# Adding the two softmaxes of a differential attention inside PSUM instead of on VectorE

## The chip, the cores and the metric

One core of a Trainium2 chip runs the whole program. The metric is the device time of one execution in microseconds (us). Of the kernel before there are three timed runs, with a median of 3167.21 us (3165.14 to 3172.83), and one profiled execution.

## The reference

The program is one inference step of a two-layer decoder whose mixer has four parallel branches. This document is about branch A, differential attention over the 2048 tokens of the prompt, with 4 heads. Each head has two queries and two keys of 32 dimensions and one value of 64:

```
def probs(q, k):
    s = einsum('bqhd,bkhd->bhqk', q, k) * scale
    return softmax(where(visible, s, NEG_BIG), axis=-1)
p = probs(q1, k1) - lam * probs(q2, k2)
return einsum('bhqk,bkhd->bqhd', p, v)
```

The result is normalised by its root mean square over the 64 values, multiplied by a gate, and goes with the other three branches through an output projection (1024 by 1024) and a LayerNorm.

## The kernel before

Each of the two layers runs in two stages. The first makes all projections and the branches B, C and D, and writes queries, keys and values of A to DRAM scratch. The second stage is `attention` together with `out_tile`, the output projection. The second stage is what the change touches.

**Tiles.** The 2048 queries are 16 query tiles of 128. They go in blocks of 4, 4, 4, 2 and 2 tiles; within a block the loops run over 4 heads and then over the tiles of the block. A query tile number qi sees qi + 1 key tiles of 128, so a head has 1 + 2 + ... + 16 = 136 pairs of query tile and key tile, and the program has 136 x 4 heads x 2 layers = 1088. There are 16 x 4 x 2 = 128 calls of `attn_probs`, one per layer, head and query tile. A call with more than 8 key tiles works in two pieces (a first piece of 1024 keys, and the rest); 64 of the 128 calls do.

**attn_probs**, for each of the two softmaxes (m = 0, 1) and each piece: TensorE forms the scores in PSUM (L678, with a mask matmul L680 on the diagonal), VectorE takes the row maximum (L682, and L684 takes the smaller of the negated maxima of both pieces), ScalarE takes the exponential into an SBUF tile P1 or P2 with the row sum beside it (L686). The rows are not divided by their sum: since the output is normalised afterwards, only the ratio of the two sums matters, and VectorE forms it as one factor per row, r = -lam * l1 / l2 (L697, L698). Where there are two pieces, the first one needs a further factor per row, col(0, 5) for m = 0 and col(1, 5) for m = 1 (L691). Then the two tiles are added on VectorE into P1: for the last piece P1 += r * P2 (L712); for the first of two pieces ScalarE scales P2 (L706, after a one-column product L702) and VectorE adds it to the scaled P1 (L707).

**attn_value** takes P1 in groups of up to 4 key tiles. TensorE transposes each 128 x 128 part into PSUM (L725, `nc.tensor.transpose` with the identity), ScalarE copies the group to SBUF (L727), and TensorE multiplies it with the values into an accumulator (L730, on one of two 64-column halves of the array). After the last tile of a block TensorE adds the two halves (L741) and the head is normalised.

**Order.** `attention` emits `attn_probs` of a tile before `attn_value` of the tile before it, so one tile's probabilities are in the making while the last one's are multiplied. After a block's attention the program emits `out_tile` for the tiles of the block before (L1373 to L1375, three fp32r matmuls for each of 8 parts and 2 halves). A scheduler of the framework then fixes the order of each engine's instructions; each engine works through its own list in order. The P1 tiles come from 5 buffers and the P2 tiles from 3 (`NP1`, `NP2`), the scores from two PSUM buffers of 1024 columns, the transposed groups from two PSUM banks. A buffer is taken again when its last reader is done.

Of the kernel before, what the change touches and what calls it, by code (L numbers as in the profile page):

```python
# [9 lines left out]
F32 = mybir.dt.float32  # L10
# [4 lines left out]
AF = mybir.ActivationFunctionType  # L15
ALU = mybir.AluOpType
# [8 lines left out]
P = 128  # L25
# [43 lines left out]
def hymba_step_kernel(  # L69
# [9 lines left out]
    nc = tc.nc  # L79
# [9 lines left out]
    RW = TG + NS  # L89
    NB = TG // 512  # L90

    KN = dict(zs=5, ms=2, os=4, NK=5, NMW=8, APO='o k p2 h p1 v v0 op q', ORD0='g10 n1 g2 b4 g4 n1', ORD1='g8 n2',
              NPH=2, NP1=5, NP2=3, LEAD=1, KD0=0, KD1=1, LO0=2, LO1=2, ZIP=0, WF=0, RUN=1, QB=0, RB=0, RC=0, RD=1, RS=1,
              RA=0, RO=0, GP=1, CI=1, CS=0, MO=0, PT=300, PSA=0, PN=1000, PB=0, PG=0, PD=1000, PBV=0, PCZ=0, PGB=0,
              POUT=-500, PATT=0, PMOD=0, PW=0, PAV=0, PDZ=3000, PQK=500, PSL=0, PSLD=0, PPR=0, PPB=0, OT=1, GO=0, DO=0,
              EP2=0, ECB=0, EPH=0, EAS=0, EAV=0, EDV=0, EOH=0, EOL=1, EOT=1, ESH=0, ESL=1, EQK=1, EDN=1, EAN=1, EDB=1,
# [8 lines left out]

    pick = lambda k: nc.gpsimd if KN[k] else nc.vector

    def cpy(k, out, in_):

        (nc.vector.tensor_copy if KN[k] else nc.scalar.copy)(out, in_)  # L110
    NST = dict(zs=KN['zs'], ms=KN['ms'], os=KN['os'])
    NK, NMW, NPH, NP1, NP2, LEAD = (KN[k] for k in ('NK', 'NMW', 'NPH', 'NP1', 'NP2', 'LEAD'))
    APO, ORD0, ORD1 = (KN[k].split() for k in ('APO', 'ORD0', 'ORD1'))
    PT, PSA, PN, PB, PG = (KN[k] for k in ('PT', 'PSA', 'PN', 'PB', 'PG'))

# [18 lines left out]
    def nm(s):  # L134
        uid[0] += 1
        return f"{s}_{uid[0]}"
# [4 lines left out]
    def St():  # L141
        return pS.tile([P, 1024], F32, tag="S", name=nm("S"))

    def Tt():
        pool.t2 = not pool.t2
        return (pool.T2 if pool.T2 and pool.t2 else pT).tile([P, 512], F32, tag="T", name=nm("T"))
# [4 lines left out]
    def st(tag, dt=F32):  # L151

        return stp.tile([P, 512], dt, tag=tag, name=nm(tag), bufs=NST[tag])
# [4 lines left out]
    def sm(who, kind="", bufs=4):  # L158
        n = SW[who]
        return smp.tile([P, n], I32 if kind == "i" else F32, tag="sm" + who + kind, name=nm("sm" + who + kind), bufs=bufs)  # L160
# [39 lines left out]
    ident = cst[:, C_ID:C_ID + 128]  # L200
# [462 lines left out]
    def attn_probs(qi, qt, kst, l1, Lx, ap):  # L663

        nk = qi + 1
        npc = -(-nk // 8)
        stt = smp.tile([P, 16], F32, tag="stt", name=nm("stt"), bufs=3)
        Pm = []
        sizes = [min(8, nk - k0) * P for k0 in range(0, nk, 8)]
        col = lambda m, j: stt[:, m * 8 + j:m * 8 + j + 1]  # L670
        for m in range(2):
            pms = []
            for pc, n in enumerate(sizes):
                s = St()
                for o in range(0, n, 512):
                    w = min(512, n - o)
                    diag = pc == npc - 1 and o + 512 >= n
                    nc.tensor.matmul(s[:, o:o + w], qt[:, m, :], kst[pc * 2 + o // 512][:, m, 0:w], start=True, stop=not diag)  # L678
                    if diag:
                        nc.tensor.matmul(s[:, o + w - P:o + w], identb, cmaskb, start=False, stop=True)  # L680

                nc.vector.tensor_reduce(col(m, pc), s[:, :n], AX.X, ALU.max, negate=True)  # L682
                if pc:
                    nc.vector.tensor_tensor(col(m, pc), col(m, pc), col(m, 0), ALU.min)  # L684
                p = (ap.p1, ap.p2)[m].tile([P, 1024], F32, tag=("P1", "P2")[m], name=nm("P"), bufs=(NP1, NP2)[m])
                nc.scalar.activation(p[:, :n], s[:, :n], AF.Exp, bias=col(m, pc), scale=1.0, accum_out=l1 if m == 0 and npc == 1 else col(m, 2 + pc))  # L686
                pms.append(p)
            lt = l1 if m == 0 and npc == 1 else col(m, 2)
            if npc > 1:

                nc.scalar.activation(col(m, 5), col(m, 0), AF.Exp, bias=col(m, 1), scale=-1.0)  # L691
                lt = col(m, 6) if m else l1
                nc.vector.scalar_tensor_tensor(lt, col(m, 2), col(m, 5), col(m, 3), op0=ALU.mult, op1=ALU.add)
            Pm.append((pms, lt))
        (p1s, lt1), (p2s, lt2) = Pm
        r = col(0, 7)
        nc.vector.reciprocal(r, lt2)  # L697
        nc.vector.scalar_tensor_tensor(r, lt1, Lx.nlam, r, op0=ALU.mult, op1=ALU.mult)  # L698
        for pc, n in enumerate(sizes):
            p1, p2 = p1s[pc], p2s[pc]  # L700
            if pc == 0 and npc > 1:
                nc.vector.tensor_tensor(col(1, 7), col(1, 5), r, ALU.mult)  # L702
                if KN['EP2']:
                    nc.gpsimd.tensor_scalar(p2[:, :n], p2[:, :n], col(1, 7), None, op0=ALU.mult)
                else:
                    nc.scalar.activation(p2[:, :n], p2[:, :n], AF.Copy, scale=col(1, 7))  # L706
                nc.vector.scalar_tensor_tensor(p1[:, :n], p1[:, :n], col(0, 5), p2[:, :n], op0=ALU.mult, op1=ALU.add)  # L707
            elif n <= KN['ECB'] * P:
                nc.scalar.activation(p2[:, :n], p2[:, :n], AF.Copy, scale=r)
                nc.gpsimd.tensor_tensor(p1[:, :n], p1[:, :n], p2[:, :n], ALU.add)  # L710
            else:
                nc.vector.scalar_tensor_tensor(p1[:, :n], p2[:, :n], r, p1[:, :n], op0=ALU.mult, op1=ALU.add)  # L712
        return p1s

    def attn_value(qi, pm, vst, acc, ls, j4, nt, hd, act, Lx, l, ap):

        nk = qi + 1
        hs = slice(hd * 64, (hd + 1) * 64)
        for c in range(0, nk, 4):
            n = min(4, nk - c)  # L720
            p1 = pm[c // 8]
            o = (c % 8) * P
            pt = Tt()
            for j in range(n):
                nc.tensor.transpose(pt[:, j * P:(j + 1) * P], p1[:, o + j * P:o + (j + 1) * P], ident)  # L725
            ph = ap.h.tile([P, 4, P], F32, tag="ph", name=nm("ph"), bufs=NPH)
            (nc.vector.tensor_copy if n <= KN['EPH'] else nc.scalar.copy)(ph[:, 0:n].rearrange("p k q -> p (k q)"), pt[:, 0:n * P])  # L727
            for j in range(n):
                e = (c + j) % 2
                nc.tensor.matmul(acc[e * 64:(e + 1) * 64, j4 * P:(j4 + 1) * P], vst[c // 4][:, j, hs], ph[:, j, :],  # L730
                                 start=(c + j < 2), stop=(c + j >= nk - 2), tile_position=(0, e * 64))
        if nk == 1:
            nc.vector.memset(acc[64:128, 0:P], 0.0)
        if j4 < nt - 1:
            return
        asb = ap.o.tile([P, 512], F32, tag="asb", name=nm("asb"), bufs=1)
        cpy('EAS', asb[:, 0:nt * P], acc[:, 0:nt * P])

        pt = Tt()
        for j in range(nt):  # L740
            nc.tensor.matmul(pt[:, j * 64:(j + 1) * 64], asb[:, j * P:(j + 1) * P], diagm, start=True, stop=True)  # L741
        ot = ap.o.tile([P, 4, 64], F32, tag="ot", name=nm("ot"), bufs=1)[:, 0:nt]
        nc.scalar.copy(ot, pt[:, 0:nt * 64].rearrange("p (a v) -> p a v", v=64))
        sq = st("ms")[:, 0:nt * 64].rearrange("p (a b) -> p a b", b=64)
        nc.scalar.activation(sq, ot, AF.Square)
        ss, l2, lt = sm("a")[:, 0:nt], sm("a")[:, 0:nt], ls[:, 0:nt]
        nc.vector.tensor_reduce(ss, sq, AX.X, ALU.add)
        nc.vector.scalar_tensor_tensor(l2, lt, EPS, lt, op0=ALU.mult, op1=ALU.mult)
        nc.vector.scalar_tensor_tensor(ss, ss, 1.0 / 64.0, l2, op0=ALU.mult, op1=ALU.add)
        ss = rsqrt(ss, P, nt, "a", KN["RA"] and act is None)  # L750
        on3 = st("ms")[:, 0:nt * 64].rearrange("p (a b) -> p a b", b=64)
        nc.vector.tensor_tensor(on3, ot, ss.unsqueeze(2).to_broadcast([P, nt, 64]), ALU.mult)
        if act is not None:
            nc.vector.tensor_tensor(act[:, :, hs], on3, Lx.ag.unsqueeze(1).to_broadcast([P, nt, 64]), ALU.mult)
            return
        pick('EAN').tensor_tensor(on3, on3, Lx.ag.unsqueeze(1).to_broadcast([P, nt, 64]), ALU.mult)
        store(tok_rows(scr[l].cat, qi - nt + 1, nt)[:, hd * 64:(hd + 1) * 64].rearrange("(t p) c -> p t c", p=P), on3)
# [651 lines left out]
    for l in range(DEPTH):  # L1409
        with ExitStack() as ctx2:  # L1410
# [3 lines left out]
            for g in range(NG):  # L1414
# [3 lines left out]
                with tc.tile_pool(name=nm("dp"), reuse_waits="tile", bufs=1) as dp:  # L1418
                    d_init(g, Sx, dp)
                    if g == 0:  # L1420
                        h, bh = build_h(l, 0, Lx)
# [31 lines left out]
                with tc.tile_pool(name=nm("cn"), reuse_waits="tile", bufs=1) as C.pool:  # L1453
# [38 lines left out]
                    if g < NG - 1:  # L1492
                        prio(PB, run, bh)
                        h = hn
# [7 lines left out]
        with ExitStack() as ctx2, \  # L1502
                tc.tile_pool(name=nm("pz"), reuse_waits="tile", bufs=1, space=PSUM) as pool.z, tc.tile_pool(name=nm("pT"), reuse_waits="tile", bufs=1, space=PSUM) as pool.T2:
            ap = L()
            for n in APO:
                setattr(ap, n, ctx2.enter_context(tc.tile_pool(name=nm("ap" + n), reuse_waits="tile", bufs=1)))
            op = ap.op
# [67 lines left out]
```

## Time and profile before

| | before |
|---|---|
| median of three runs | 3167.21 us |
| the profiled execution's own time | 3160.83 us |
| its span, first to last instruction | 3159.1 us |
| mean granted TensorE clock | 0.951 |
| attention stage, layer 0 | 1029 to 1600 us |
| attention stage, layer 1 | 2573 us to the end |

How to read the profile: PE is TensorE's matmuls, PEld its weight loads, DVE VectorE, ACT ScalarE, POOL GpSimd, SP the queue that issues DMAs. A group of instructions has its source line, engine, operation, output and inputs by the program's names, shapes, a count, then the busy time and the mean time of one in ns, then the idle time ahead of them on their engine and what ended most of it. Matmuls are pipelined: each has a recorded length, but the next may begin long before it ends, so the distance between two starts tells what one costs, and busy time does not. A matmul of fp32 numbers that is no transpose shows as two records in the trace, each with a weight load of its own: L741 runs 128 times and has 256 records.

### The profile page before, as it was taken

The numbers are of one execution on the slowest core, as the hardware profiler recorded it, in microseconds if no ns is written. First come the engines' busy times: TensorE is split into PE (matmuls) and PEld (weight loads), VectorE is DVE, ScalarE is ACT, GpSimd is POOL, SyncE is SP. The second block draws the span as 40 slices with busy tenths as digits, with TensorE's granted clock in tenths as the row PEclk, the third lists the DMA queues.
The fourth block names the chain that finished last, engine by engine and source line by source line (L and its number), as shares of the span: only waits on it lengthen the run. The fifth ranks groups of instructions, "written<-read, shape, count | busy, mean of one in ns | idle before, by whom it ended". The sixth has DMA issues, their size and how long they took to land. (4 is left out here: it accounts for less than half of the span.)

```text
span 3159.1 us, 55749 instructions
## 1 busy us (share of the span) xinstructions
PE 2828.0 (90%) x20888; PEld 2254.7 (71%) x20888; DVE 2235.2 (71%) x5280; ACT 1162.9 (37%) x2452; POOL 960.8 (30%) x1061
## 2 busy tenths in 40 slices
PE   5999989898999798888979999999999988997986
PEld 3888876788876566656668888767888856665665
DVE  2567883367583788879956678833676749898897
ACT  3212223211112666666641112232110146567663
POOL 3344364312011233404253344552120031332232
PEclk8999999899999899989989999999999988998998
DMA  6433544323555754446453335444334355444652
GB/s 237 147 128 108 173 146 154 108 92 128 174 180 203 184 133 112 118 112 166 122 197 111 122 119 192 140 139 124 117 120 140 117 166 123 129 118 108 158 155 67
DMA packets 323263, 441.31 MB, mean 140 GB/s; under 512 B 58704, under 2 KB 207734, under 8 KB 315811
## 3 DMA queue, kind: packets, MB, share of 16 engines
q1 hardware_dynamic: 316850, 420.97, 44.0%
q0 software_dynamic: 6144, 16.79, 1.8%
q8 instruction: 165, 2.70, 0.4%
q14 instruction: 104, 0.84, 0.1%
HBM read 295.80 MB, written 142.05 MB: 139 GB/s over the span
## 5 line engine op out<-in xcount | busy, mean ns | idle before, releaser
L525 PE MATMUL z<-hh,wh 128*128 128x512 f32 (+1 forms) x1440 | 528.4, 367 | 17.1 <-DVE zs L195 9.1
L527 PE MATMUL z<-hh,wl 128*128 128x512 f32 (+1 forms) x1440 | 522.1, 363 | 0.0
L526 PE MATMUL z<-hl,wh 128*128 128x512 f32 (+1 forms) x1440 | 518.6, 360 | 0.0
L516 PE MATMUL z<-wh,hh 128*128 128x256 f32 (+1 forms) x1360 | 399.9, 294 | 16.0 <-ACT wh L110 4.3
L686 ACT ACTIVATE P<-S,stt 128x1024 f32<-128x1024 f32 (+7 forms) x384 | 332.7, 868 | 182.1 <-DVE stt L682 120.0
L518 PE MATMUL z<-wh,hl 128*128 128x256 f32 (+1 forms) x1360 | 394.7, 290 | 0.0
L517 PE MATMUL z<-wl,hh 128*128 128x256 f32 (+1 forms) x1360 | 393.9, 290 | 0.6 <-POOL wl L172 0.6
L682 DVE TENSOR_REDUCE stt<-S 128x1 f32<-128x1024 f32 (+7 forms) x384 | 344.0, 904 | 64.2 <-PE S L680 48.7
L1026 DVE SCALAR_TENSOR_TENSOR acc<-glu,cw,acc 128x512 f32<-128x512 f32 x480 | 378.0, 834 | 3.3
L525 PEld LDWEIGHTS z<-hh,wh 128*128 128x128 f32 x1440 | 275.7, 191 | 80.1 <-issue 14.4
L527 PEld LDWEIGHTS z<-hh,wl 128*128 128x128 f32 x1440 | 275.5, 191 | 44.7 <-issue 7.0
L526 PEld LDWEIGHTS z<-hl,wh 128*128 128x128 f32 x1440 | 275.7, 191 | 42.7 <-issue 6.3
L678 PE MATMUL S<-K,Q 128*128 128x512 f32 (+3 forms) x640 | 229.2, 430 | 77.1 <-ACT P L686 61.6
L516 PEld LDWEIGHTS z<-wh,hh 128*128 128x128 f32 (+1 forms) x1360 | 262.3, 193 | 25.9 <-issue 5.7
L517 PEld LDWEIGHTS z<-wl,hh 128*128 128x128 f32 (+1 forms) x1360 | 261.9, 193 | 4.9 <-issue 2.6
L518 PEld LDWEIGHTS z<-wh,hl 128*128 128x128 f32 (+1 forms) x1360 | 261.5, 192 | 2.3 <-issue 0.3
L172 POOL TENSOR_TENSOR wl<-raw,wh 128x512 fp32r<-128x512 f32 x112 | 150.8, 1362 | 256.5 <-ACT wh L110 218.2
L1373 PE MATMUL z<-woh,zs 128*128 128x512 f32 (+1 forms) x480 | 202.7, 422 | 24.0 <-ACT zs L110 15.1
L1375 PE MATMUL z<-woh,zs 128*128 128x512 f32 (+1 forms) x480 | 200.2, 417 | 10.0 <-POOL zs L172 9.8
L730 PE MATMUL X<-ph,V 128*64 128x128 f32 x2176 | 196.1, 294 | 10.4 <-ACT ph L727 9.8
L678 PEld LDWEIGHTS S<-K,Q 128*128 128x128 f32 x640 | 114.9, 204 | 122.1 <-ACT P L686 90.0
L725 PE MATMUL T<-cst,P 128*128 128x128 f32 x1088 | 189.2, 302 | 13.3 <-DVE P L707 8.8
(374 smaller groups left out, 5410.5 us busy)
## 6 DMA issues: line engine op xcount, KB each, us to landing
wp<-wh SPq DMA_DIRECT2D x28, 1024.0 KB
wp<-wl SPq DMA_DIRECT2D x28, 1024.0 KB
wh<-wp SPq DMA_DIRECT2D x56, 512.0 KB
wl<-wp SPq DMA_DIRECT2D x56, 512.0 KB
K<-kh SPq DMA_DIRECT2D x224, 128.0 KB
K<-kl SPq DMA_DIRECT2D x224, 128.0 KB
mw<-in_w_ada_dram SPq DMA_DIRECT2D x24, 1024.0 KB
raw<-in_w_in_dram SPq DMA_DIRECT2D x64, 256.0 KB
```

Source lines behind the costliest of these rows:

```text
L516: nc.tensor.matmul(ps, hh[:, k, tok:tok + M], wh[:, k, :], start=(k == 0), stop=False)
L517: nc.tensor.matmul(ps, hh[:, k, tok:tok + M], wl[:, k, :], start=False, stop=False)
L518: nc.tensor.matmul(ps, hl[:, k, tok:tok + M], wh[:, k, :], start=False, stop=(k == KT - 1))
L525: nc.tensor.matmul(ps, wh[:, k, ms], hh[:, k, c0:c0 + n], start=(k == 0), stop=False)
L526: nc.tensor.matmul(ps, wh[:, k, ms], hl[:, k, c0:c0 + n], start=False, stop=False)
L527: nc.tensor.matmul(ps, wl[:, k, ms], hh[:, k, c0:c0 + n], start=False, stop=(k == KT - 1))
L678: nc.tensor.matmul(s[:, o:o + w], qt[:, m, :], kst[pc * 2 + o // 512][:, m, 0:w], start=True, stop=not diag)
L682: nc.vector.tensor_reduce(col(m, pc), s[:, :n], AX.X, ALU.max, negate=True)
L686: nc.scalar.activation(p[:, :n], s[:, :n], AF.Exp, bias=col(m, pc), scale=1.0, accum_out=l1 if m == 0 and npc == 1 else col(m, 2 + pc))
L1026: nc.vector.scalar_tensor_tensor(av, src(j), Lx.cw[:, c, j:j + 1], av, op0=ALU.mult, op1=ALU.add)
L1373: nc.tensor.matmul(po[0:M], a, wh[:, k, :], start=(i == 0), stop=False)
L1375: nc.tensor.matmul(po[0:M], b, wh[:, k, :], start=False, stop=(i == KT - 1))
```

## The change

The two P tiles are no longer added on VectorE. `attn_probs` returns both, with a pair of 128 x 128 fp32 matrices for each piece: for the last piece the identity and `dr`, the identity times r; for a first piece two diagonal matrices with the factors of P1 and P2. VectorE makes them with one instruction each (the identity times one or two columns): `dr` in each of the 128 calls, from one buffer, and a pair in each of the 64 calls with two pieces, from two buffers. `attn_value` replaces each transpose by two fp32 matmuls that accumulate in PSUM: P1's part times its matrix, then P2's part times its own. The sum of both is the transposed, combined part. The P buffers become 4 and 4. The tile `asb`, the accumulator's copy, moves from a buffer of its own to the ring `ms` of two buffers.

```diff
-    KN = dict(... APO='o k p2 h p1 v v0 op q', ... NP1=5, NP2=3, ...
+    KN = dict(... APO='o k p2 h p1 v v0 op q dg', ... NP1=4, NP2=4, ...
...
-        for pc, n in enumerate(sizes):
-            p1, p2 = p1s[pc], p2s[pc]
-            if pc == 0 and npc > 1:
-                nc.vector.tensor_tensor(col(1, 7), col(1, 5), r, ALU.mult)
...
-                    nc.scalar.activation(p2[:, :n], p2[:, :n], AF.Copy, scale=col(1, 7))
-                nc.vector.scalar_tensor_tensor(p1[:, :n], p1[:, :n], col(0, 5), p2[:, :n], op0=ALU.mult, op1=ALU.add)
...
-                nc.vector.scalar_tensor_tensor(p1[:, :n], p2[:, :n], r, p1[:, :n], op0=ALU.mult, op1=ALU.add)
-        return p1s
+        dr = ap.dg.tile([P, P], F32, tag="dr", name=nm("dr"), bufs=1)
+        nc.vector.tensor_scalar(dr, ident, r, None, op0=ALU.mult)
+        diag = [(ident, dr)]
+        if npc > 1:
+            d2 = ap.dg.tile([P, 2, P], F32, tag="dg", name=nm("dg"), bufs=2)
+            nc.vector.tensor_scalar(d2[:, 0], ident, col(0, 5), None, op0=ALU.mult)
+            nc.vector.tensor_scalar(d2[:, 1], ident, col(1, 5), r, op0=ALU.mult, op1=ALU.mult)
+            diag.insert(0, (d2[:, 0], d2[:, 1]))
+        return p1s, p2s, diag
...
-            p1 = pm[c // 8]
+            p1s, p2s, diag = pm
...
-                nc.tensor.transpose(pt[:, j * P:(j + 1) * P], p1[:, o + j * P:o + (j + 1) * P], ident)
+                ks, js = slice(o + j * P, o + (j + 1) * P), slice(j * P, (j + 1) * P)
+                for m, p in enumerate((p1s[c // 8], p2s[c // 8])):
+                    nc.tensor.matmul(pt[:, js], p[:, ks], diag[c // 8][m], start=(m == 0), stop=(m == 1))
...
-        asb = ap.o.tile([P, 512], F32, tag="asb", name=nm("asb"), bufs=1)
+        asb = st("ms")
```

## Rows read from the trace of the kernel before

**Rows 1.** The page's first part: engine, busy us, share, count
```profile
PE 2828.0 (90%) x20888; PEld 2254.7 (71%) x20888; DVE 2235.2 (71%) x5280; ACT 1162.9 (37%) x2452; POOL 960.8 (30%) x1061
```

**Rows 2.** Busy time of each engine in stretches: both attention stages
```profile
core 0: us, PE busy (x) PEld busy (x) DVE busy (x) ACT busy (x) POOL busy (x), PEclk, DMA share, GB/s
1029.00:1600.00 571.00, 490.16 (x3027) 354.35 (x3028) 486.85 (x1234) 358.97 (x777) 174.22 (x137) 0.93 0.52 135
2573.00:3159.00 586.00, 502.10 (x3084) 360.96 (x3082) 501.95 (x1255) 359.75 (x772) 159.48 (x125) 0.93 0.47 124
```

**Rows 3.** The same view: projections, then two stretches within attention
```profile
800.00:1000.00 200.00, 199.09 (x1039) 147.36 (x1038) 124.16 (x245) 27.46 (x47) 11.59 (x4) 1.00 0.52 179
1550.00:1575.00 25.00, 23.12 (x151) 16.80 (x150) 24.57 (x51) 15.76 (x30) 10.61 (x7) 1.00 0.24 74
1325.00:1400.00 75.00, 57.62 (x374) 41.01 (x375) 60.81 (x160) 57.42 (x124) 7.70 (x7) 0.84 0.44 103
```

**Rows 4.** Groups by line, whole span: VectorE and ScalarE instructions that are removed
```profile
L712 DVE SCALAR_TENSOR_TENSOR P<-P,stt,P 128x128 f32<-128x128 f32 (+7 forms) x128 | 113.7, 889 | 0.4
L707 DVE SCALAR_TENSOR_TENSOR P<-P,stt,P 128x1024 f32<-128x1024 f32 x64 | 87.7, 1371 | 9.2 <-ACT P L706 9.0
L706 ACT ACTIVATE P<-P,stt 128x1024 f32<-128x1024 f32 x64 | 73.6, 1150 | 25.5 <-DVE stt L702 25.5
L702 DVE TENSOR_TENSOR stt<-stt 128x1 f32<-128x1 f32 x64 | 19.4, 303 | 0.8
```

**Rows 5.** Groups by line, whole span: TensorE's work of the attention stages
```profile
L678 PE MATMUL S<-K,Q 128*128 128x512 f32 (+3 forms) x640 | 229.2, 430 | 77.1 <-ACT P L686 61.6 <-DMA K<-kl 10.1 <-DMA K<-kh 3.4
L1373 PE MATMUL z<-woh,zs 128*128 128x512 f32 (+1 forms) x480 | 202.7, 422 | 24.0 <-ACT zs L110 15.1 <-DVE t L1377 8.3
L1373 PE MATMUL S<-woh,zs 128*128 128x512 f32 x64 | 29.4, 459 | 6.0 <-ACT zs L110 3.9 <-DVE t L1377 1.9 <-ACT P L686 0.2
L730 PE MATMUL X<-ph,V 128*64 128x128 f32 x2176 | 196.1, 294 | 10.4 <-ACT ph L727 9.8
L725 PE MATMUL T<-cst,P 128*128 128x128 f32 x1088 | 189.2, 302 | 13.3 <-DVE P L707 8.8 <-DVE P L712 3.2 <-ACT ot L743 1.1
L741 PE MATMUL T<-cst,asb 128*128 128x64 f32 x256 | 35.8, 279 | 1.9 <-ACT asb L110 1.9
L1354 PE MATMUL z<-cst,os 128*128 128x128 f32 (+1 forms) x128 | 20.6, 282 | 11.7 <-DVE t L1377 8.2 <-ACT zs L998 2.1 <-DMA os<-cat 1.3
```

**Rows 6.** TensorE's timeline at full clock: start us, us, instruction, count
```profile
1227.30 0.66 PE L730 MATMUL X<-ph,V 128*64 128x128 f32 x8 [0.29 <-ACT ph L727]
1227.89 0.66 PE L725 MATMUL T<-cst,P 128*128 128x128 f32 x4
...
1242.01 0.39 PE L1375 MATMUL z<-woh,zs 128*128 128x512 f32 x1
...
1243.14 0.40 PE L1374 MATMUL z<-wol,zs 128*128 128x512 f32 x1
1243.38 1.00 PE L741 MATMUL T<-cst,asb 128*128 128x64 f32 x8
1244.22 0.61 PE L725 MATMUL T<-cst,P 128*128 128x128 f32 x4
```

**Rows 7.** Timeline of the first stage: one full fp32 matmul, 128 columns moving, two records
```profile
252.28 0.44 PE L1242 MATMUL S<-di,ckE 128*128 128x128 f32 x2
```

**Rows 8.** Groups by line and shape, VectorE: nearest to the new diagonal builds
```profile
L1136 DVE TENSOR_SCALAR dfs<-dfs 128x64 f32<-128x64 f32 x4 | 0.8, 195 | 0.1
L474 DVE TENSOR_SCALAR zs<-S,sc1T,shT 128x128 f32<-128x128 f32 x32 | 12.4, 407 | 8.9 <-PE S L460 7.7 <-DMA Q<-qh 0.4
L417 DVE TENSOR_SCALAR Z<-sgb,smp,vT 128x64 f32<-128x64 f32 x8 | 4.7, 1358 | 0.0
```

More of the change, by code (lines that the diff above doesn't have):

```diff
@@ L90, in hymba_step_kernel @@
     NB = TG // 512
-    KN = dict(zs=5, ms=2, os=4, NK=5, NMW=8, APO='o k p2 h p1 v v0 op q', ORD0='g10 n1 g2 b4 g4 n1', ORD1='g8 n2',
-              NPH=2, NP1=5, NP2=3, LEAD=1, KD0=0, KD1=1, LO0=2, LO1=2, ZIP=0, WF=0, RUN=1, QB=0, RB=0, RC=0, RD=1, RS=1,
+    KN = dict(zs=5, ms=2, os=4, NK=5, NMW=8, APO='o k p2 h p1 v v0 op q dg', ORD0='g10 n1 g2 b4 g4 n1', ORD1='g8 n2',
+              NPH=2, NP1=4, NP2=4, LEAD=1, KD0=0, KD1=1, LO0=2, LO1=2, ZIP=0, WF=0, RUN=1, QB=0, RB=0, RC=0, RD=1, RS=1,
               RA=0, RO=0, GP=1, CI=1, CS=0, MO=0, PT=300, PSA=0, PN=1000, PB=0, PG=0, PD=1000, PBV=0, PCZ=0, PGB=0,
@@ L698, in attn_probs @@
         nc.vector.scalar_tensor_tensor(r, lt1, Lx.nlam, r, op0=ALU.mult, op1=ALU.mult)
-        for pc, n in enumerate(sizes):
-            p1, p2 = p1s[pc], p2s[pc]
-            if pc == 0 and npc > 1:
-                nc.vector.tensor_tensor(col(1, 7), col(1, 5), r, ALU.mult)
-                if KN['EP2']:
-                    nc.gpsimd.tensor_scalar(p2[:, :n], p2[:, :n], col(1, 7), None, op0=ALU.mult)
-                else:
-                    nc.scalar.activation(p2[:, :n], p2[:, :n], AF.Copy, scale=col(1, 7))
-                nc.vector.scalar_tensor_tensor(p1[:, :n], p1[:, :n], col(0, 5), p2[:, :n], op0=ALU.mult, op1=ALU.add)
[L708 to L711, printed above, removed]
-                nc.vector.scalar_tensor_tensor(p1[:, :n], p2[:, :n], r, p1[:, :n], op0=ALU.mult, op1=ALU.add)
-        return p1s
+        dr = ap.dg.tile([P, P], F32, tag="dr", name=nm("dr"), bufs=1)
[7 more added lines that the diff above has]
+        return p1s, p2s, diag
     def attn_value(qi, pm, vst, acc, ls, j4, nt, hd, act, Lx, l, ap):
```

## The prediction

> **What bounds the kernel now.** I read the page first: TensorE is busy 90% of the span, VectorE 71% [rows 1]. That is an average over two stages, and the change lies in one of them, so the next view is the busy time by stretches. The two attention stages take 571 + 586 = 1157 us; in them VectorE is busy 486.85 + 501.95 = 989 us (85%), TensorE's matmuls 992 us, ScalarE 719 us [rows 2]. Busy time alone leaves two candidates. Two things separate them. The waits ahead of TensorE's score matmuls end on ScalarE's exponentials (61.6 us), those ahead of its transposes on VectorE's additions L707 and L712 [rows 5]: TensorE waits for the softmax, not the other way round. And its records overlap: a record is about 0.28 us long (L741's mean of 279 ns [rows 5]), but starts lie closer. So I count starts. In the timeline [rows 6] four transposes L725 fit in 0.61 us, a pitch of (0.61 - 0.28) / 3 = 0.11 us; eight records of L741 in 1.00 us, 0.103; five output-projection matmuls start within 1.13 us, 0.226 each; a group of eight L730 ends 0.59 us after it began, when the next begins, 0.074 each.
>
> TensorE's need at full clock, with the counts of [rows 5] (L1374 and L1375 have the counts of L1373): output projection 3 x (480 + 64) x 0.226 = 369 us; scores 640 x 0.226 = 145, taken as if all were 512 wide; L730 2176 x 0.074 = 160; transposes 1088 x 0.11 = 120; L741 256 x 0.103 = 26; L1354 128 x 0.11 = 14. Sum 834 us, 72% of the stage, with 323 us to spare. VectorE reaches 24.57 of 25 us in its best stretch [rows 3]. It bounds most of the stage, helped by places where everything waits on the chain: from 1325 to 1400 us TensorE's granted clock is 0.84 [rows 3].
>
> **What is taken away.** VectorE loses L712 (113.7 us), L707 (87.7) and L702 (19.4): 221 us. ScalarE loses L706, 73.6 us [rows 4]; ScalarE at 62% bounds nothing, so that is worth only its place in the chain. A call with two pieces no longer runs L702, L706, L707 in series, 0.30 + 1.15 + 1.37 = 2.8 us, between the factor r and its first transpose. Since one tile's probabilities are made while the last one's are multiplied, this shortens a delay that is partly hidden; I give nothing for it.
>
> **What VectorE gets.** 128 builds of `dr` and 2 for each of 64 calls: 256 tensor_scalar instructions of 128 x 128 fp32. The trace has none exactly like it. Below is L1136, 128 x 64, at 195 ns; above is L417, 128 x 64, at 1358 ns; the same shape is L474 at 407 ns, though from PSUM [rows 8]. I take 407 for its shape: 104 us, with ends 50 and 348. VectorE's net is -117 us (-171 to +127).
>
> **What TensorE gets.** Each of the 1088 pairs had one transpose of one record; it gets two fp32 matmuls that are not transposes, of two records each like L741's: four records for one. L741 loads the same 128 x 128 weights and moves 64 columns at a pitch of 0.103. L1242 is the full form, 128 columns moving, but stands alone: two records in 0.44 us, a distance of 0.44 - 0.28 = 0.16 [rows 7]. In a stream of 16 records for a group I expect L741's neighbourhood and take 0.11. Added: 1088 x 3 x 0.11 = 359 us (at 0.103: 1088 x (0.412 - 0.11) = 329; at 0.16: 577). All of it is on one engine with 323 us to spare. TensorE's need becomes 834 + 359 = 1193 us, 36 more than the stage has today, and VectorE's falls to 872. **The bound moves to TensorE.**
>
> A rule of the Trainium skill makes this dearer: "TensorE: Matmul & The Clock Gate", section Terms, says that transpose mode is four times faster for fp32, so a plain fp32 matmul would cost four transposes. The rows give two (two records at 0.103 to 0.11 against one at 0.11); the rule's sum is a rival below.
>
> **How full TensorE gets.** No engine works every microsecond of its bound. Today's bound engine has 85% of the stage; TensorE in a projection stretch has 199.09 of 200 us [rows 3]. I take 95%, nearer to TensorE's own figure: a third of its need is output projection that waits for no softmax, and what it waits for today, VectorE, gets 117 us lighter. 1193 / 0.95 = 1256, 99 more than 1157. Ends: 1163 / 0.995 = 1169 (+12) with the cheap pitch; 1193 / 0.85 = 1404 (+247).
>
> **New waits.** P2 used to be free after VectorE's addition and is now held until TensorE has read it. Four and four buffers are two calls of two pieces, so the exponentials of the call after next wait for TensorE's last reads, and behind that L686 stand ScalarE's copies L727 for the same TensorE. While TensorE is the bound this is its own lateness handed round, covered in the 95%. `dr` has one buffer: its next build on VectorE waits for the last matmul that reads the old one, with row maxima and output-tile work queued behind it in VectorE's order. `asb` shares a ring of two with the head's norm, once per head and block; cover is the next head's scores, and without it the cost is 40 copies. No DMA is added, removed or moved, and SP's and POOL's queues are passed by nothing.
>
> **The sum.** 3160.8 (the profiled execution's own time) + 99 = 3260; the median lies 6 us above that execution, so 3266 us, 3% slower.
>
> **Rivals.**
> One: the single buffer of `dr` adds to that. After each call's last read come a build (0.41) and a record's length (0.28) before the next call's P2 matmuls can go on: 128 x 0.69 = 88 us, 3266 + 88 = 3354. It decides if TensorE's list has no score or projection matmuls to put there. Against it: today's order puts them between such groups.
> Two, faster: VectorE stays the bound, because TensorE hides the added records. The place is the pitch: L730's eight records in 0.66 us start (0.66 - 0.28) / 7 = 0.054 apart. At that pitch 1088 x (0.216 - 0.11) = 115 us are added, TensorE needs 949, and the stage is VectorE's 872 at today's 85%: 1020, 137 less, 3030 us. It decides below a pitch of 0.102, where the 323 us suffice. Against it: L730 loads 64 columns, half the array; no row with 128 fp32 weight columns is under 0.103.
> Three: pitch near 0.10 and TensorE nearly always full; it comes out even, 3167.
> Four: a matmul costs four transposes. Then 1088 x (8 x 0.11 - 0.11) = 838 us are added, 1672 / 0.95 = 1760, 3770 us. That is the skill's figure from Terms above. Against it: L741's records.
>
> **How the numbers follow.** Forecast 0.72, rival one 0.14, two 0.06, three 0.05, four 0.03. The range goes from just above the cheap end, 3185, to 3370, which is a fill of 88% (1193 / 0.88 = 1356, +199) and takes in rival one; outside lie two, three, four and little of the forecast. A measurement of this kernel can tell about 0.3%, 9.5 us, from no change. Faster by more: rival two and a scrap of three, 0.07. Within: 0.05. Slower: 0.88; the forecast's own range is 3200 to 3350.
>
> **What would show it.** In the changed kernel L712, L707, L706 and L702 are gone, a group of matmuls into the transposed tile has 4352 records at a pitch of 0.11 us, VectorE's busy time in the attention stages falls by about 117 us, and both stages get longer, by some 50 us each; before 1029 us and between the stages nothing moves. ScalarE's copies wait longer for TensorE, VectorE's row maxima for scores. TensorE's granted clock there rises from 0.93 if it is kept full. The forecast is wrong if the pitch is under 0.10, if VectorE still ends most waits, or if TensorE is idle over a tenth of the stage.

## The result, and the profile after

The changed kernel takes 3357.02 us (median of four, 3341.32 to 3358.41) against 3170.02 us of the kernel before run beside it: a ratio of 1.058, 95% interval 1.0544 to 1.0616. The forecast was 3266 us in a range of 3185 to 3370; the direction was right, the size near the range's upper end: 187 us more where 99 were forecast.

The page's first part, against [rows 1], and two more lines of it. "PEclk" is the granted clock in tenths of full speed over 40 slices of the span (9 is 90% or more). The last line is the chain of work that ended last, followed back through the span, with each engine's share of it:

```profile
PE 3139.7 (94%) x24152; PEld 2602.1 (78%) x24152; DVE 2114.4 (63%) x5280; ACT 1107.4 (33%) x2388; POOL 945.4 (28%) x1061
PEclk7999999899999999999989999899999999999999
PE 73%; DVE 15%; DMA 4%; issue 3%; POOL 3%; ACT 2%; SPq 1%; DVEq 0%; ACTq 0%; POOLq 0%
```

TensorE has 24152 - 20888 = 3264 more records, which is 1088 x 3, as worked out. VectorE's count is the same by chance: 256 instructions went (128 + 64 + 64) and 256 came.

The two attention stages, against [rows 2]:

```profile
core 0: us, PE busy (x) PEld busy (x) DVE busy (x) ACT busy (x) POOL busy (x), PEclk, DMA share, GB/s
1036.00:1690.00 654.00, 637.23 (x4645) 520.56 (x4645) 427.21 (x1226) 328.07 (x739) 147.69 (x128) 0.99 0.45 116
2681.00:3356.00 675.00, 652.61 (x4716) 531.48 (x4714) 441.52 (x1256) 331.11 (x740) 147.34 (x126) 0.99 0.42 109
```

They take 654 + 675 = 1329 us, 172 more than the 1157 of before. VectorE's busy time fell from 989 to 869 us, TensorE's rose from 992 to 1290, and its granted clock from 0.93 to 0.99, with fewer waits ahead of its matmuls. The other 25 us of the span's 197 lie outside (7 before the first stage, 18 between the two, with nearly the same count of instructions); two runs of this one kernel differ by 17, and I did not follow them up.

Groups by line, against [rows 4] and [rows 5] (lower down in the kernel, lines after the change are three lower: L722 was L725, L724 was L727, L727 was L730):

```profile
L722 PE MATMUL T<-dg,P 128*128 128x128 f32 x2048 | 268.2, 281 | 0.0
L722 PE MATMUL T<-cst,P 128*128 128x128 f32 x1152 | 238.8, 290 | 0.0
L722 PE MATMUL T<-dr,P 128*128 128x128 f32 x1152 | 226.7, 280 | 4.8 <-DVE dr L701 4.4 <-DVE smo L1380 0.4
L678 PE MATMUL S<-K,Q 128*128 128x512 f32 (+3 forms) x640 | 204.1, 397 | 6.7 <-DMA K<-kl 3.9 <-ACT P L686 2.2
L682 DVE TENSOR_REDUCE stt<-S 128x1 f32<-128x1024 f32 (+7 forms) x384 | 342.4, 907 | 136.7 <-PE S L680 83.6 <-PE S L678 51.4
L686 ACT ACTIVATE P<-S,stt 128x1024 f32<-128x1024 f32 (+7 forms) x384 | 332.0, 866 | 304.4 <-DVE stt L682 186.1 <-PE T L722 43.2 <-DVE stt L684 32.6
L724 ACT COPY ph<-T 128x512 f32<-128x512 f32 (+2 forms) x320 | 163.5, 521 | 211.4 <-PE T L722 208.0 <-PE S L680 3.1
L701 DVE TENSOR_SCALAR dr<-cst,stt 128x128 f32<-128x128 f32 x128 | 52.6, 411 | 91.9 <-PE T L722 91.1
L705 DVE TENSOR_SCALAR dg<-cst,stt 128x128 f32<-128x128 f32 x64 | 25.9, 404 | 2.8 <-ACT stt L691 2.1 <-PE T L722 0.6
L706 DVE TENSOR_SCALAR dg<-cst,stt 128x128 f32<-128x128 f32 x64 | 25.7, 402 | 1.4
```

Two of these lines in the kernel before:

```profile
L682 DVE TENSOR_REDUCE stt<-S 128x1 f32<-128x1024 f32 (+7 forms) x384 | 344.0, 904 | 64.2 <-PE S L680 48.7 <-PE S L678 13.5
L727 ACT COPY ph<-T 128x512 f32<-128x512 f32 (+2 forms) x320 | 160.1, 522 | 103.2 <-PE T L725 101.8 <-PE S L680 0.4
```

Before, the waits went both ways; now they go almost all one way. The score matmuls L678 waited 61.6 us for exponentials [rows 5] and now wait 2.2. VectorE's wait for TensorE ahead of the row maxima rose from 62 to 135 us, with 91 more ahead of the next `dr`; that of ScalarE's copies rose from 102 to 208. TensorE's timeline (start us, length, instruction, count) shows no hole:

```profile
1302.42 2.05 PE L722 MATMUL T<-dg,P 128*128 128x128 f32 x16
1304.23 0.48 PE L1370 MATMUL z<-woh,zs 128*128 128x512 f32 x1
...
1307.28 0.39 PE L1371 MATMUL z<-wol,zs 128*128 128x512 f32 x1
1307.60 0.66 PE L727 MATMUL X<-ph,V 128*64 128x128 f32 x8
1308.19 0.49 PE L722 MATMUL T<-cst,P 128*128 128x128 f32 x2
```

Sixteen records of L722 begin at 1302.42 and what follows begins at 1304.23: 0.113 us each.

### The profile page after: what moved, and what is told of

It reads as the page before. It is cut to its first block, busy times and chain, and to the rows that moved or that the text cites. A ratio compares the mean times of both kernels' runs of the same rounds, so it can differ in the third digit from the quotient of the medians.

```text
span 3356.6 us, 62147 instructions
## 1 busy us (share of the span) xinstructions
PE 3139.7 (94%) x24152; PEld 2602.1 (78%) x24152; DVE 2114.4 (63%) x5280; ACT 1107.4 (33%) x2388; POOL 945.4 (28%) x1061
## 4 chain that ended last, share of the span: by engine, by line
PE 73%; DVE 15%; DMA 4%; issue 3%; POOL 3%; ACT 2%; SPq 1%; DVEq 0%; ACTq 0%; POOLq 0%
PE T L722 15%; PE z L525 7%; PE z L527 7%; PE z L526 7%; PE X L727 5%; DVE acc L1023 4%; PE S L678 4%; PE z L516 3%; PE z L517 3%; PE z L518 3%; PE z L1370 3%; PE z L1372 3%; PE z L1371 3%; DVE catt L1184 1%; PE S L1150 1%
## 5 line engine op out<-in xcount | busy, mean ns | idle before, releaser
L686 ACT ACTIVATE P<-S,stt 128x1024 f32<-128x1024 f32 (+7 forms) x384 | 332.0, 866 | 304.4 <-DVE stt L682 186.1
L682 DVE TENSOR_REDUCE stt<-S 128x1 f32<-128x1024 f32 (+7 forms) x384 | 342.4, 907 | 136.7 <-PE S L680 83.6
L722 PE MATMUL T<-dg,P 128*128 128x128 f32 x2048 | 268.2, 281 | 0.0
L722 PEld LDWEIGHTS T<-dg,P 128*128 128x128 f32 x2048 | 244.0, 192 | 19.8 <-issue 17.5
L722 PE MATMUL T<-cst,P 128*128 128x128 f32 x1152 | 238.8, 290 | 0.0
L724 ACT COPY ph<-T 128x512 f32<-128x512 f32 (+2 forms) x320 | 163.5, 521 | 211.4 <-PE T L722 208.0
L722 PE MATMUL T<-dr,P 128*128 128x128 f32 x1152 | 226.7, 280 | 4.8 <-DVE dr L701 4.4
L172 POOL TENSOR_TENSOR zs<-os,zs 128x512 fp32r<-128x512 f32 (+1 forms) x64 | 79.6, 1246 | 480.3 <-ACT zs L110 339.1
```

The lines of the kernel that those rows point to most:

```text
L172: eng.tensor_tensor(out, x, hi.bitcast(F32), ALU.subtract)
L722: nc.tensor.matmul(pt[:, js], p[:, ks], diag[c // 8][m], start=(m == 0), stop=(m == 1))
```

## The experiments

Each was timed beside the kernel before, and ratios are against that. Four groups: what bounded the kernel before, what the added records cost, what else the change brings, and whether cheaper records turn it round. With each edit the scheduler also puts TensorE's matmuls into a somewhat different order (with the buffer counts alone, too), and the times include that.

**What bounded before.** No addition at all, on the kernel before:

```diff
-        for pc, n in enumerate(sizes):
...
-                nc.vector.scalar_tensor_tensor(p1[:, :n], p2[:, :n], r, p1[:, :n], op0=ALU.mult, op1=ALU.add)
         return p1s
```

> The kernel before without any addition of the two softmaxes: the instructions of L702, L706, L707 and L712 are left out, and P1 alone goes on to the transposes, so the second softmax is missing from the output. TensorE's list is as before (one transpose record per pair). If VectorE bounded the attention stages before (my theory), 221 us of its 989 us are gone and TensorE's 834 us remain: the stage at 90% to 95% of one engine is 880 to 930 us, so 2900 to 2950 us in all. If TensorE or the chain of scores and exponentials was the bound already, the time falls by less than 100 us, to above 3070.

Measured: 3056.59 us, ratio 0.9653 (0.9626 to 0.9679), 113 less. Between the two, and much nearer to the rival: 107 us above my range, 13 below the rival's bound. Without 221 us of VectorE and 74 of ScalarE the program loses about half of VectorE's part; and as the transposes here wait neither for r nor for P2, not all of the 113 us need be VectorE's relief. The stretches of both attention stages in this kernel:

```profile
1038.00:1568.00 530.00, 484.39 (x3113) 354.05 (x3112) 405.24 (x1138) 334.18 (x766) 173.40 (x145) 0.97 0.59 157
2528.00:3058.00 530.00, 479.58 (x3084) 349.79 (x3082) 401.44 (x1128) 325.42 (x740) 151.23 (x126) 0.96 0.52 137
```

VectorE is down to 807 of 1060 us (76%), with TensorE's records covering 91% of it. So VectorE was a bound before, with TensorE close behind, and not the only one. The waits of before said so too: VectorE stood 62 us ahead of its row maxima L682 for TensorE.

The counterpart adds TensorE work alone:

```diff
-                nc.tensor.transpose(pt[:, j * P:(j + 1) * P], p1[:, o + j * P:o + (j + 1) * P], ident)
+                nc.tensor.matmul(pt[:, j * P:(j + 1) * P], p1[:, o + j * P:o + (j + 1) * P], ident, start=True, stop=True)
```

> The kernel before, with each transpose written as a plain fp32 matmul with the identity: 1088 more records on TensorE, 1088 x 0.112 = 122 us, and nothing else. My theory (VectorE bounds before, TensorE has idle time): most of it is hidden, the time rises by 10 to 50 us, to 3180 to 3220. The rival that TensorE was as much the bound before: it rises by 100 to 130 us, to 3270 to 3300. In both the pitch of the new records is 0.112 us; if a plain fp32 matmul cost four transposes, 1088 x 3 x 0.112 = 366 us would be added and the time would be over 3350.

Measured: 3195.79 us, ratio 1.0088 (1.0059 to 1.0117), 26 more. The first 1088 added records cost 0.024 us each instead of their pitch: most of them go into TensorE's idle time. A group of this kernel's timeline:

```profile
1272.82 2.00 PE L725 MATMUL T<-cst,P 128*128 128x128 f32 x16
```

With records 0.28 us long, (2.00 - 0.28) / 15 = 0.115 from start to start.

**What the last records cost.** In the changed kernel, a transpose opens the accumulation where P1's factor is the identity:

```diff
                 for m, p in enumerate((p1s[c // 8], p2s[c // 8])):
-                    nc.tensor.matmul(pt[:, js], p[:, ks], diag[c // 8][m], start=(m == 0), stop=(m == 1))
+                    if diag[c // 8][m] is ident:
+                        nc.tensor.matmul(pt[:, js], p[:, ks], ident, start=True, stop=False, is_transpose=True)
+                    else:
+                        nc.tensor.matmul(pt[:, js], p[:, ks], diag[c // 8][m], start=(m == 0), stop=(m == 1))
```

> The changed kernel, with the identity's term of the last piece (576 of the 1088 pairs) as a transpose of one record that opens the accumulation, and P2's matmul added to it as before: 576 records fewer on TensorE. My theory: 576 x 0.112 = 65 us less of the bound engine, 3280 to 3305 us. A rival in which waits and not records set the time: 3345 to 3365, no change.

Measured: 3290.29 us, ratio 1.0398 (1.0366 to 1.0431): 66.7 us less than the change for 576 records fewer, 0.116 each, the full pitch as near as it can be told (the change's own runs differ by 17 us, 0.03 for each record). At this end a record counts in full, which is what a saturated engine means:

```profile
L723 PE MATMUL T<-cst,P 128*128 128x128 f32 x576 | 166.8, 291 | 0.0
L725 PE MATMUL T<-dr,P 128*128 128x128 f32 x1152 | 208.4, 281 | 2.8 <-DVE dr L701 2.2 <-DVE smo L1383 0.5
```

The identity's term has 576 records in place of 1152, the other is as it was.

The two halves of the change, first pieces alone and last pieces alone (the latter with the transpose that opens, and with two buffers for `dr`):

```diff
-        diag = [(ident, dr)]
+        diag = [None]
+        n = sizes[-1]
+        nc.vector.scalar_tensor_tensor(p1s[-1][:, :n], p2s[-1][:, :n], r, p1s[-1][:, :n], op0=ALU.mult, op1=ALU.add)
...
+                if diag[c // 8] is None:
+                    nc.tensor.transpose(pt[:, js], p1s[c // 8][:, ks], ident)
+                    continue
```

> Half of the change: only the first pieces (512 of the 1088 pairs) are added in PSUM, with four records for one; the last pieces keep VectorE's addition L712 and the transpose. TensorE gets 512 x 0.336 = 172 us, VectorE loses L707 and L702 (107 us) and gets 128 diagonal builds (52 us), ScalarE loses L706 (74 us). My theory, that TensorE's spare time in the attention stages before was some 250 us and is used up last: about even, 3130 to 3180 us. A rival in which any pair combined in PSUM costs its full price: 512/1088 of the change's 187 us, 88 us more, 3255.

```diff
-            d2 = ap.dg.tile([P, 2, P], F32, tag="dg", name=nm("dg"), bufs=2)
...
+            nc.scalar.activation(p2[:, :n], p2[:, :n], AF.Copy, scale=col(1, 7))
+            nc.vector.scalar_tensor_tensor(p1[:, :n], p1[:, :n], col(0, 5), p2[:, :n], op0=ALU.mult, op1=ALU.add)
+            diag.insert(0, None)
```

> The other half: only the last pieces (576 pairs) are added in PSUM, as a transpose that opens the accumulation and one matmul, three records for one; the first pieces keep L702, L706, L707. TensorE gets 576 x 0.224 = 129 us, VectorE loses L712 (114 us) and gets 128 builds (52 us). My theory: it fits in TensorE's spare time, 3120 to 3170 us. The rival of a full price for each added record: 129 us more less what VectorE gives, 3230 or more.

Measured: 3237.26 us, ratio 1.0205 (1.0158 to 1.0252), and 3211.92, ratio 1.0119 (1.007 to 1.0167). Both miss my expectation on the high side, by 57 and 42 us, and each ends 18 us below its rival, so nearer to the full price than to my free one. Against the kernel before, in order of records added:

| kernel | records added | time added, us | per added record, us |
|---|---|---|---|
| plain matmul for the transpose | 1088 | 26 | 0.024 |
| last pieces only | 1152 | 40 | 0.035 |
| first pieces only | 1536 | 65 | 0.043 |
| change, opened by a transpose | 2688 | 121 | 0.045 |
| the change | 3264 | 187 | 0.057 |

The time added rises faster than the number of records, with the full 0.116 between the last two; the rows also differ in VectorE's work, so the last column is no pure price. What surprised me is the first three: by the prices above, VectorE has 62 and 55 us less to do in the second and third than in the first, and it buys nothing that shows.

**What else the change brings.** One buffer for `dr`:

```diff
-        dr = ap.dg.tile([P, P], F32, tag="dr", name=nm("dr"), bufs=1)
+        dr = ap.dg.tile([P, P], F32, tag="dg", name=nm("dr"), bufs=5)
...
-            d2 = ap.dg.tile([P, 2, P], F32, tag="dg", name=nm("dg"), bufs=2)
+            da, db = (ap.dg.tile([P, P], F32, tag="dg", name=nm("dg"), bufs=5) for _ in range(2))
```

> The changed kernel with one ring of five 128 x 128 buffers for all diagonal matrices, in place of one buffer for the last piece's matrix and two pairs for the first piece's. My theory, that the added records fill TensorE: no change, 3345 to 3365 us. The rival that the single buffer's round between VectorE and TensorE costs time: 128 x 0.69 = 88 us less, about 3270.

Measured: 3343.64 us, ratio 1.0567 (1.0536 to 1.0598), nearly the interval of the change itself, and 13 us below its median, where its own runs differ by 17. The wait is there, and more buffers do move it away, but it cost little or no time:

```profile
L701 DVE TENSOR_SCALAR dr<-cst,stt 128x128 f32<-128x128 f32 x128 | 45.8, 358 | 2.2
L682 DVE TENSOR_REDUCE stt<-S 128x1 f32<-128x1024 f32 (+7 forms) x384 | 343.4, 906 | 186.7 <-PE S L680 130.9 <-PE S L678 53.4
```

VectorE's idle time ahead of `dr` falls from 91.9 us to 2.2 and the kernel is as slow: ahead of the row maxima it rises from 136.7 to 186.7. VectorE waited for an engine that was late anyway.

VectorE's old work put back into the changed kernel:

```diff
+        for pc, n in enumerate(sizes):
+            p1 = p1s[pc]
+            nc.vector.scalar_tensor_tensor(p1[:, :n], p1[:, :n], 1.0, p1[:, :n], op0=ALU.mult, op1=ALU.max)
         dr = ap.dg.tile([P, P], F32, tag="dr", name=nm("dr"), bufs=1)
```

> The changed kernel with as much work put back on VectorE as it had before: one two-operand instruction over each piece of P1 that leaves its values as they are, ahead of the diagonal builds (some 220 us of VectorE, in the chain of each call as L707 and L712 were). My theory, that TensorE bounds the attention stages after the change and VectorE's relief is worth nothing there: less than 25 us more, 3345 to 3380. The rival that the relief is worth what was taken off: 100 us or more, over 3450.

Measured: 3392.02 us, ratio 1.0687 (1.0649 to 1.0726): 35 us more for this:

```profile
L702 DVE SCALAR_TENSOR_TENSOR P<-P 128x1024 f32<-128x1024 f32 (+2 forms) x192 | 186.0, 972 | 45.6 <-ACT P L686 44.4
```

186 us of VectorE, in the chain, are worth 35. That is above my 25 and far from the rival's 100: VectorE's work is not free there, but it is no longer what sets the time.

P1's matmul alone, P2's left out:

```diff
-                for m, p in enumerate((p1s[c // 8], p2s[c // 8])):
-                    nc.tensor.matmul(pt[:, js], p[:, ks], diag[c // 8][m], start=(m == 0), stop=(m == 1))
+                nc.tensor.matmul(pt[:, js], p1s[c // 8][:, ks], diag[c // 8][0], start=True, stop=True)
```

> The changed kernel with P2's matmul left out: each pair has P1's plain fp32 matmul alone (2176 records), so the second softmax is missing from the output. VectorE's diagonal builds stay; P2 is free again as soon as its exponential is done. If the count of records sets the time, this is near the other kernels of some 2200 records: 3190 to 3240 us. The rival that P2's longer stay in its four buffers is what holds the two halves of the change up: 3080 to 3140 us.

Measured: 3189.99 us, ratio 1.0054 (1.0027 to 1.0081). With 2176 records it stands beside the plain matmul for the transpose (3195.79, also 2176), though VectorE and ScalarE have been relieved and P2 is free early. P2's stay in its buffers is not what keeps this kernel up, and so hardly what holds the halves up, where it was not tried apart.

The buffer counts alone, on the kernel before:

```diff
-              NPH=2, NP1=5, NP2=3, ...
+              NPH=2, NP1=4, NP2=4, ...
```

> The kernel before with four P1 and four P2 buffers, in place of five and three, and nothing else. Buffers do not matter in my theory: 3160 to 3185 us. The rival that the fifth P1 buffer carries the overlap: 20 us more or above.

Measured: 3177.47 us, ratio 1.002 (1.0001 to 1.0038). On the kernel before, the counts are worth 0.2%, by the interval 0.4% at most. The other small part of the change, `asb` in the ring `ms`, was not tried apart; TensorE has no idle time ahead of the matmuls that read it (L738, 0.0 us; L741 before, 1.9).

**Cheaper records.** The same change in fp32r, one record for each matmul:

```diff
-                p = (ap.p1, ap.p2)[m].tile([P, 1024], F32, ...
+                p = (ap.p1, ap.p2)[m].tile([P, 1024], F32R, ...
...
-        diag = [(ident, dr)]
+        diag = [(identr, dr)]
```

> The changed kernel with P1, P2 and the diagonal matrices rounded to fp32r, so that each of the two matmuls of a pair is one record in place of two (2176 records for 4352; the probabilities and r lose low bits; the diagonals come from one ring of four). My theory, that the count of records sets the time: TensorE gets 1088 x 0.112 = 122 us over the kernel before, not 359, and VectorE and ScalarE keep what they were relieved of: between the kernel without any addition (3057) and before, 3070 to 3130 us. A rival in which the new order and buffers cost time whatever the records are: above 3250.

Measured: 3234.66 us, ratio 1.0189 (1.0139 to 1.024): 122 us below the change, but 105 above the expectation's upper end, between my theory and its rival, and 45 above P1's matmul alone, which has as many records. The stretches show one thing that neither had. Two of this kernel:

```profile
1250.00:1300.00 50.00, 49.25 (x316) 38.99 (x315) 39.75 (x115) 26.72 (x64) 17.64 (x15) 1.00 0.47 128
1375.00:1400.00 25.00, 21.60 (x102) 17.22 (x103) 12.65 (x40) 13.29 (x30) 1.82 (x2) 0.50 0.52 124
```

and the second one in the changed kernel:

```profile
1375.00:1400.00 25.00, 25.00 (x192) 20.88 (x192) 15.26 (x36) 13.34 (x32) 5.67 (x5) 1.00 0.49 122
```

The granted clock of the two stages is 0.88 and 0.87, and in some stretches 0.50, the lower level of 1.2 GHz, with half as many matmuls done. There the same records cost twice: sixteen in 3.65 us of this timeline, against sixteen in 1.90 us at 1303 us, at full clock.

```profile
1389.87 1.01 PE L680 MATMUL S<-K,Q 128*128 128x512 f32 x2 [2.59 <-ACT P L688]
...
1390.77 3.65 PE L724 MATMUL T<-dg,P 128*128 128x128 f32 x16
```

The wait of 2.59 us for ScalarE comes too late to have brought the clock down: from 1350 to 1375 us it is at 0.77 already. The changed kernel has no such stretch (0.99 in both stages); in the kernel before the 0.84 of [rows 3] is a mean of short stretches at the lower level and long ones at full clock. Read like that, a mean of 0.87 to 0.88 puts about a quarter of the stages, some 330 us, at the lower level, where P1's matmul alone with its 0.96 has under 100. That is enough to cover the 45 us between the two, but that it does was not tested, and why this kernel's clock falls further was not settled. The profiled execution is also the slowest of its four (0.925 over the whole span; the others have 0.934 to 0.939). In bf16:

```diff
-                p = (ap.p1, ap.p2)[m].tile([P, 1024], F32, ...
+                p = (ap.p1, ap.p2)[m].tile([P, 1024], BF16, ...
...
-        diag = [(ident, dr)]
+        diag = [(identb, dr)]
```

> The changed kernel with P1, P2 and the diagonal matrices in bf16 (the probabilities and r keep 8 bits): one record for each matmul, with the shorter weight load that the mask matmul L680 shows (103 ns recorded, against 191 for fp32). My theory: the 2176 records cost about 0.06 us each, 130 us, no more than the 1088 transposes of before (122), so this comes near the kernel without any addition: 3050 to 3120 us. A rival in which the change costs time apart from TensorE's records (buffers held longer, the lower granted clock that the fp32r kernel had): 3180 or more.

Measured: 3115.16 us, ratio 0.9822 (0.9788 to 0.9855), faster than both kernels, at the price of 8-bit probabilities. Its timeline:

```profile
1306.08 0.83 PE L722 MATMUL T<-dg,P 128*128 128x128 bf16 x12
1306.72 0.47 PE L1372 MATMUL z<-woh,zs 128*128 128x512 f32 x1
```

Twelve records in 0.64 us to the next start, 0.053 each, half of fp32's. The same additions in PSUM, VectorE's same relief, and the sign has turned. VectorE and ScalarE are as busy over the attention stages as in the changed kernel (888 and 668 us against 887 and 670); TensorE's records cover 995 us in place of 1314. So the change fails by what its records cost TensorE. Some 58 us over the kernel without any addition remain. With more buffers:

```diff
-              NPH=2, NP1=4, NP2=4, ...
+              NPH=2, NP1=6, NP2=6, ...
```

> The bf16 kernel with the room that bf16 frees given to buffers: six P1, six P2, three for each set of diagonal matrices. If the handing over of buffers between VectorE, ScalarE and TensorE is what keeps that kernel above the one without any addition (3115 against 3057): 3060 to 3090 us. If it is the 104 us of diagonal builds on VectorE and the waits on the chain of scores and maxima: 3105 to 3125, no change.

Measured: 3153.47 us beside 3200.4 of the kernel before in the same set of runs, ratio 0.985 (0.9825 to 0.9875): by the ratios, no gain over the bf16 kernel's 0.9822.

## Why the prediction was right, and what it mis-sized

- **The records.** "Four records for one", at 0.11 us: 4352 records at 0.113 in a full group. Right. The Trainium skill's factor of four ("TensorE: Matmul & The Clock Gate", section Terms) does not show here: a plain fp32 matmul is two records of a transpose's pitch, and putting one in place of the transpose cost 26 us, where a factor of four would have asked for 366 of TensorE. With it rival four falls, too.
- **VectorE.** -117 us forecast, 989 - 869 = -120 measured; the 256 builds were put at 104 us and take 52.6 + 25.9 + 25.7 = 104.2. That this came out to the microsecond is in part luck: the row it was taken from reads PSUM, and with a ring of five the same build of `dr` took 0.36 us in the mean, not 0.41.
- **The bound moves to TensorE.** Shown by the turned waits, by 0.116 us for each of the last 576 records, and by the old VectorE work put back for 35 us. The premise was too simple: "TensorE waits for the softmax, not the other way round" left out the 62 us that VectorE's row maxima and the 102 that ScalarE's copies waited for TensorE before.
- **New waits.** The exponentials do wait for TensorE's last reads of the P tiles, 43 us ahead of L686, on an engine that is busy for half of the stages. As forecast, this is TensorE's lateness handed round.
- **How full TensorE gets: the term that was mis-sized.** I divided a need of 1193 us by 95% and got 1256; the stages take 1329, so 1193 is 90% of them, and each stage is 83 to 89 us longer, not some 50. It is not mainly idleness: TensorE's records cover 1290 of the 1329 us (97%), and in 39 us none runs. My price list was too clean. Summed from each start to the next, from 1029 to 1700 us and from 2675 us on (so that the whole of the output projection that falls to these stages is in), L722 takes 520 us (479 in my list), the output projection 398 (369), L727 173 (160), scores 156 (145), L1351 26 (14), L738 30 (26), and the mask matmuls L680, which I left out, 23. Together 1326 against 1193, and 63 of the 133 were covered by the 5%. Such a sum holds idle time as well, so it tells a price only where there is little of it, as here. Prices read off the tightest groups of a timeline are floors, and a saturated engine pays the mean. With these means TensorE's need before was, as an estimate, 936 us (L725 at L722's 0.12): 81% of the stages and not 72%, and the spare 221 us and not 323.
- **The range.** That 3357 lies in it is partly luck. The forecast's own range was 3200 to 3350; the stated one reached to 3370 to take in rival one, whose 3354 is the nearest figure of all, and whose cause is refuted below.
- **Nothing for a lighter VectorE.** I took its relief as worth something in the 95%, as I took VectorE for the bound before. The kernel without any addition says at most half: 113 us for 221, with ScalarE's 74 and the wait for r and P2 gone too. TensorE was so near the bound that the two halves of the change did not pay either.
- **Rivals.** The single buffer of `dr` (0.14) is refuted: its wait went and the time stayed within 13 us, where 88 were asked for. A VectorE that stays the bound (0.06) and a break-even (0.05) asked for a pitch of about 0.10 or less, and it was 0.113. Rival two's 3030 us for a cheap pitch was too low as well: the bf16 kernel, with two records at 0.053 for each pair where the rival had four at 0.054, takes 3115.

Three kernels with about 2200 transposing records (plain matmul, last pieces, P1 alone) lie within 3190 to 3212 us however much VectorE has to do. The stretches tell which engine holds them there. From the first score matmul of a layer to its last output-projection matmul, both layers together:

| kernel | stages, us | TensorE's records cover, us | not covered, us | VectorE busy, us |
|---|---|---|---|---|
| before | 1179 | 1011 | 168 | 1000 |
| no addition | 1055 | 962 | 93 | 805 |
| P1 alone | 1198 | 1101 | 97 | 887 |
| plain matmul for the transpose | 1210 | 1111 | 99 | 984 |
| last pieces only | 1228 | 1111 | 117 | 943 |
| the change | 1360 | 1314 | 46 | 887 |

TensorE's part is the same in the three, 1101 to 1111 us, while VectorE's goes from 887 to 984: there TensorE sets the time. Further records go in part into what is still uncovered, 46 us in the change. The step from no addition (3057 us) to P1's matmul alone (3190), 0.122 us for each of 1088 records, is 139 us more of TensorE's records and 4 of uncovered time, so TensorE is not left idle longer by the matmuls' wait for the diagonal builds. What stays open is why some 100 us stay uncovered in these kernels, and why a lighter VectorE does not shorten them.

## What to carry to other kernels

Before moving work from one engine to another, sum the other engine's need in that stage, with every small group in it, at mean distances from start to start taken where that engine is hardly kept waiting, and not at those of the tightest groups; 72% by clean prices was some 81% by mean ones. Read the waits in both directions, too: here VectorE and ScalarE waited for TensorE while TensorE waited for them. Folding an addition into a PSUM accumulation is cheap only when the matmul that carries it is: it replaced one record by four in fp32 and by two half-price ones in bf16, and in these runs that decided the sign.

## What was not expected of the hardware

- A matmul on half of the columns did not follow one on all of them at once. After the output-projection matmul at 1307.28, L727 starts 0.32 us later, where the next of its own kind starts 0.23 us later; after the eight L727, which start within 0.4 us, L722 begins 0.59 us after the first. The step from an L1372 of 512 columns to L727 has the same 0.32 us as its median over both stages.
- An fp32 transpose can open an accumulation that a plain matmul then adds to; the trace shows it as one record with a shorter weight load (82.2 us busy for 576, 143 ns each, against 192 for the plain matmuls' in the same kernel):

```profile
L725 PEld LDWEIGHTS T<-dg,P 128*128 128x128 f32 x2048 | 245.2, 192 | 22.0 <-issue 16.4 <-DVE dg L706 3.6
L723 PEld LDWEIGHTS T<-cst,P 128*128 128x128 f32 x576 | 82.2, 143 | 26.8 <-issue 26.8
```

- Half the records on TensorE (fp32r) came with a lower granted clock in the same stages, 0.88 and 0.87 against 0.99, which can have given back part of what they saved; P1's plain fp32 matmul alone, with as many records, had 0.96.
